# Four edits of order in a hybrid decoder trunk: a weight load's priority, two loads and casts hung behind others, and the bank of two sets of transposes

## The chip, the cores and the metric

The kernel runs on 1 core of one Trainium2 chip. The metric is the device time of one execution in microseconds. The core's engines are named as the profile names them: PE (TensorE, matmuls and transposes; PEld are its weight loads), DVE (VectorE), ACT (ScalarE), POOL (GpSimd) and SP (SyncE), whose queue issues the DMAs here.

## The reference, cut to what matters

One step of a two-layer decoder trunk for 1024 prompt tokens and 8 samples of one token each, D = 1024, in float32:

```python
def trunk(x, p, ...):
    h = x
    for i in range(DEPTH):                       # 2 layers
        hn = rmsnorm(h, norm_mix[i])
        if i % 2 == 0:
            y, S = hgrn2_mixer(hn, ...)          # (o * silu(z)) @ w_out
        else:
            y, vt = chunk_mlp_mixer(hn, ...)     # (u * s * silu(z)) @ w_out, with v = layernorm(gelu(v))
        h = h + y
        gate = sigmoid(rmsnorm(h, norm_ple[i]) @ w_ple_gate[i])
        h = h + gate * (p[i] @ w_ple_proj[i])
    return rmsnorm(h, norm_final), ...
```

Outputs are the trunk's rows, the recurrent states and the normalised v rows of the open chunk.

## The kernel before, in words

Activations lie with features on the partitions. The 1032 tokens are three row blocks c = 0, 1, 2 of 384, 384 and 264 columns (`W`). A weight matrix is walked in tiles of 128 outputs and 1024 inputs. Each product is made in three matmuls (`mm3`, L234): operands are split into a high part, cast by ACT to fp32r, and a low part, the rest, by DVE or POOL; high x high, high x low and low x high are added in one PSUM bank (L236, L237, L238). So a weight tile costs a DMA into `wstg` (two buffers, and a third in some stages), a cast on ACT (`whi`, L150) and a subtraction on DVE (`wlo`, L151) before PE can use it, and two buffers each of `whi` and `wlo` hold the tile in use and the next one.

The wide matrices are done by units (`unit`, L480): a Strassen-like scheme in which two weight tiles together with sums of their quarters (`load_unit`, L185) are multiplied with sums of row blocks 0 and 1; row block 2 is done plainly. Some tiles of each matrix are done plainly throughout.

The order of the work: PE's instructions stand in the order in which the program traces them. Side work is written as generators that are advanced by ticks (`Ticks`, L48) between groups of matmuls. The instructions of the other engines and of SP's queue are ordered by the scheduler when the program is built, greedily: the instruction that is ready with the highest priority goes first. Priority is the place in the program; `tc.high_priority(offset=n)` moves it n places forward (`PRI` is 400), and `tc.issue_after(x)` adds that an instruction on x's engine stands behind x in that engine's queue, without a wait for x to finish.

`order` (L127 to L141) is the list of weight tiles; `take` (L216) hands out one and loads the next one. The places that the change touches:

- **`load` (L167 to L183)**: fetches a tile and splits it. Tiles of the second layer's input matrix ("b"), of the gates ("g") and one half of "p" have their cast and subtraction at high priority; the DMA has none of it.
- **`load_unit` (L185)**: for the first layer's output matrix the key is "Oa" and f is 0 or 1. Its two weight DMAs (L197) have high priority. The first unit, ("Oa", 2, 0), is loaded when the second plain output tile is taken.
- **`last_fill` (L1200)**: the end of the recurrent layer. It makes the second half of p's projection, then loads the gated rows of block 2 for the first half of the output projection: `load_zt` takes four pieces of two rows of 128x264 each from DRAM (`ozd`) through two buffers `zstg` (L385), with a cast (L394) and a subtraction (L398) each. It then takes the first output tile; the plain tiles 0 and 1 of the output projection follow in `out_phase` (L1245).
- **`ple` (L1418)**: the gate stage of each layer. `several(0, 2)` runs tiles 0 and 1 block by block, so that both are used before the next block; then come single tiles. At its head the rows' normalisation (`norm_proc`, L308) is still running: per row j of a block a scaling on DVE (L318), a cast on ACT (L231) and a subtraction (L232), on DVE for odd j and on POOL for even j. A block's normalisation is traced as a whole when its turn comes: block 0's before the first gate group, block 1's within it.
- **`mid` (L1530)**: called before the fourth gate tile of the first layer. It loads the second layer's p rows for all three blocks (`load_p`, L334): DMA, cast L339, subtraction L340. The casts stand behind `last["split"]`, the latest cast of a row. p is used behind the gate stage (`pple`, L352).
- **`vstore` (L1563)**: the second layer's v tiles. Each block of a tile, after its gelu (L1558), is transposed by PE (L1567) into the PSUM tile `pt_g` (tag "pt", one buffer), copied by ACT (L1569), summed for the layer norm (L1572) and stored. Tiles 0 to 3 are done plainly, in pairs block by block (L1578 to L1590), and tiles 4 and up by units. The tag "po" is a bank of its own; the normalisation's sums (`norm_sum`, L284) and the row sums `pr` (L1609) use it too.

Of the kernel before, what the change touches and what calls it, by code (L numbers as in the profile page):

```python
# [8 lines left out]
F32 = mybir.dt.float32  # L9
# [8 lines left out]
P = 128  # L18
# [12 lines left out]
PRI = 400  # L31
# [50 lines left out]
def trunk_kernel(ctx, tc, xT, st, pT, nrm, wina, lbl, gna, wouta, winb, lng, lnb, lngr, lnbr,  # L82
                 wsp, bsp, woutb, wgate, wproj, cst, msk,
                 yT, so_p, so_s, cv_p, cv_s):
    nc = tc.nc
    V, A, G, PE = nc.vector, nc.scalar, nc.gpsimd, nc.tensor
# [3 lines left out]
    def pool(stack, name, bufs=1, **kw):  # L90
        return stack.enter_context(tc.tile_pool(name=name, bufs=bufs, reuse_waits="tile", **kw))
# [5 lines left out]
    pp = pool(ctx, "psum", space=PSUM)  # L97
# [29 lines left out]
    order = [("p", 0, 0), ("a", 8), ("a", 0), ("a", 32), ("a", 33)]  # L127
# [14 lines left out]
    wsrc = {"p": wproj, "a": wina, "z": wina, "oa": wouta, "g": wgate, "b": winb, "ob": woutb}  # L142
# [4 lines left out]
    def split_weights(src, width, names, pl):  # L147
        hi = pl.tile([P, width], F32R, name=names[0], **names[2])
        lo = pl.tile([P, width], F32R, name=names[1], **names[2])
        A.copy(hi, src)  # L150
        last["wnew"] = V.tensor_tensor(lo, src, hi.bitcast(F32), ALU.subtract)  # L151
        return hi, lo

# [6 lines left out]
    def fetch_weights(n):  # L160
        src = wsrc[order[n][0]]
        for i in order[n][1:]:
            src = src[i]
        staged[n] = wp.tile([P, 1024], F32, name="wstg")
        nc.sync.dma_start(staged[n], src)

    def load(n, wait=False):  # L167
        if n >= len(order) or n in loaded or wait and order[n][0] == "B":
            return
        if order[n][0][0].isupper():  # L170
            loaded[n] = load_unit(*order[n])
            return
        if n not in staged:
            fetch_weights(n)
        stg = staged.pop(n)
        with tc.high_priority(offset=PRI if order[n][:2] == ("p", 1) or order[n][0] in ("b", "g") else 0):
            if order[n] in spare:
                hi, lo = loaded[n] = spare[order[n]]()
                split(hi, lo, stg)
            else:  # L180
                loaded[n] = split_weights(stg, 1024, PLAIN, wp)
                if order[n] == ("b", MI + 2):
                    rest["w2"] = last["wnew"]  # L183

    def load_unit(key, m, f=None):  # L185


        a = []
        for _ in range(2):

            third = key != "Z" and nst[0] % 3 == 2
            a.append(ws[0].tile([P, 1024], F32, name="wstg3", bufs=1) if third else
                     wp.tile([P, 1024], F32, name="wstg"))
            nst[0] += key != "Z"
        with tc.high_priority(offset=0 if f is None or (key, m, f) == ("Ob", 4, 0) else PRI):
            for i in range(2):
                nc.sync.dma_start(a[i], wsrc[key.lower()][m + i] if f is None else wsrc[key.lower()][m + i, f])  # L197
        a11, a12, a21, a22 = (a[i][:, j * 512:(j + 1) * 512] for i in range(2) for j in range(2))
        w0 = split_weights(a[0], 1024, PLAIN, wp)
        t = ws[0].tile([P, 512], F32, name="ssum", bufs=2)  # L200
        eng = G if key == "B" else V
        eng.tensor_tensor(t, a21, a22, ALU.add)
        s1 = split_weights(t, 512, SUMS, ws[0])
        eng.tensor_tensor(t, t, a11, ALU.subtract)
        s2 = split_weights(t, 512, SUMS, ws[0])
        t3 = ws[0].tile([P, 512], F32, name="ssum", bufs=2)
        eng.tensor_tensor(t3, a11, a21, ALU.subtract)
        s3 = split_weights(t3, 512, SUMS, ws[0])
        eng.tensor_tensor(t, a12, t, ALU.subtract)
        s4 = split_weights(t, 512, SUMS, ws[0])  # L210
        w1 = split_weights(a[1], 1024, PLAIN, wp)
        return w0, w1, (s1, s2, s3, s4)
# [15 lines left out]
    last, rest = {}, {}  # L228

    def split(hi, lo, src, eng=V):  # L230
        last["split"] = A.copy(hi, src)  # L231
        last["lo"] = eng.tensor_tensor(lo, src, hi.bitcast(F32), ALU.subtract)  # L232
# [139 lines left out]
    def load_zt(zt, parts, stage, n=2, lag=0, tie=True, behind=None):  # L372


        todo = [(ozd[c][:, k0 + k:k0 + k + n, :], *(x[:, k:k + n, :] for x in zt[c, k0][:2]), W[c])
                for c, k0 in parts for k in range(0, zt[c, k0][2], n)]
        return load_list(todo, stage, lag, tie, behind)

    def load_list(todo, stage, lag=0, tie=True, behind=None):

        stg = []
        def fetch(i):
            if i < len(todo):
                stg.append(stage(todo[i][3]))
                last["zt"] = nc.sync.dma_start(stg[i], todo[i][0])  # L385

        for i in range(len(todo) + lag):
            if not lag:
                fetch(i)
            if i >= lag:  # L390
                _, zh, zl, _ = todo[i - lag]
                first = behind and behind()
                with tc.issue_after(first.ins) if first else ExitStack():
                    hi = A.copy(zh, stg[i - lag])  # L394
                if tie:
                    tc.keep_in_program_order(hi)
                with tc.issue_after(rest["sum"].ins) if first and "sum" in rest else ExitStack():
                    V.tensor_tensor(zl, stg[i - lag], zh.bitcast(F32), ALU.subtract)  # L398

            if lag:  # L400
                fetch(i)
            yield

    def stage2(tp, bufs):
        return lambda w: tp.tile([P, 2, 384], F32, name="zstg", bufs=bufs)[:, :, :w]
# [4 lines left out]
    def run(gen):  # L410
        for _ in gen:
            pass
# [770 lines left out]
    zt = {}  # L1183
# [16 lines left out]
    def last_fill():  # L1200
        def halves_of_m():
            while True:
                yield wa.tile([P, 384], F32, name="pple_t", tag="vf", bufs=2)
                t = wa.tile([P, 2, 384], F32, name="pple_t", tag="M", bufs=2)
                yield t[:, 0, :]
                yield t[:, 1, :]

        where = halves_of_m()
        for i, y in enumerate(pple(0, ph, pl, 1, lambda c, mm: next(where)[:, :W[c]])):
            if i == 7:  # L1210
                with tc.issue_after(last["pple"].ins):
                    load(taken[0])
            yield y
        run(load_zt(zt, [(2, 0)], stage2(wa, 2), tie=False))
        assert not any(p[2].__name__ == "reload" for p in tk.procs)
        pre["w"] = take("oa", 0, 0)
        for c in (0, 1):
            pre[c] = pp.tile([P, 512], F32, name="ps_o", tag="mm", bufs=3)
            yield from out_half(pre[c], pre["w"], zt, c, 0)
# [22 lines left out]
    def new_ssq():  # L1242
        return [sp.tile([P, W[c]], F32, name=f"ssq{c}", bufs=1) for c in CH]
# [278 lines left out]
    with ExitStack() as sG:  # L1522
        ep = pool(sG, "pj")
        ssq2 = new_ssq()
        hn = new_act()
        with ExitStack() as s:
            pq = pool(s, "p1", side="right")
            ph, pl = [None] * 3, [None] * 3

            def mid():  # L1530
                behind = last["split"]
                for c in CH:
                    load_p(pq, 1, c, ph, pl, behind, [x[:, :2, :W[c]] for x in xm[c]])

            early = {}
            ple(0, ep, act[0], act[1], ssq2, lambda c: tk.spawn(norm_rows(c, ssq2, 2, (*hn, early), NDEL[1][c])), mid)
            for i, _ in enumerate(pple(1, ph, pl, 0, places([(pq, "pple_t", 8)]))):
                early.setdefault("p", last["pple"])
                if i % 2 or i > 4:
                    tk.tick()  # L1540
# [21 lines left out]

    def vstore(m, c, gv):  # L1563

        pt = pp.tile([P, 3, P], F32, name="pt_g", tag="pt", bufs=1)
        for i in range(NT[c]):
            PE.transpose(pt[:, i, :], gv[:, i * P:(i + 1) * P], ident)  # L1567
        gt = wide().rearrange("p (n e) -> p n e", e=P)
        A.copy(gt[:, :NT[c], :], pt[:, :NT[c], :])  # L1569
        n0 = OFF[c] // P  # L1570
        for i in range(NT[c]):
            V.bn_stats(stats[:, n0 + i, m, :], gt[:, i, :])  # L1572
        nc.sync.dma_start(vraw[m // 2][:, n0:n0 + NT[c], (m % 2) * P:(m % 2 + 1) * P], gt[:, :NT[c], :])
        return
        yield
# [144 lines left out]
    for g in range(8):  # L1720
# [6 lines left out]
        for c in (1, 0, 2):  # L1727
            vn[c] = wb2.tile([P, NT[c], DV], F32, name=f"vn{c}", bufs=1)
            nc.sync.dma_start(vn[c], vraw[g][:, OFF[c] // P:OFF[c] // P + NT[c]])
            for i in range(NT[c]):  # L1730
                n = OFF[c] // P + i
# [12 lines left out]
        else:  # L1744

            zt = {(0, 0): (hh[0], hl[0], 8), (1, 0): (*xm[1], 4), (1, 4): (*xm[0], 4), (2, 0): (hh[2], hl[2], 8)}
# [209 lines left out]
```

## Time and profile before

| what | value |
|---|---|
| median of 3 runs | 1835.99 us (1834.75 to 1836.6) |
| the profiled execution's own time | 1835.75 us |
| its span | 1833.5 us |
| mean granted clock of TensorE | 0.998 |
| HBM read / written | 182.82 MB / 72.80 MB |

The span runs from the first to the last instruction of the program; the execution's own time is 2.25 us longer. A timeline row gives start and duration in us, engine, source line, operation, what it writes and reads, its shape, how many were merged, and in brackets the engine's idle time before it with what ended it. A row of waits gives who waited for whom, and total, times and longest in us. A row of stretches gives the stretch, its length, the busy time and count of PE, PEld, DVE, ACT and POOL, the granted clock, the share of the DMA engines' time, and GB/s. Matmuls are pipelined and their ends are modelled: a matmul's row is longer than the distance to the next one's start, so a short stall of PE doesn't show as idle time.

### The profile page before, as it was taken

How to read it: one execution, taken by the hardware profiler on the slowest of the kernel's cores; microseconds unless marked ns; L12 is line 12 of the kernel's file. 1: busy time of each engine (PE TensorE's matmuls, PEld its weight loads, DVE VectorE, ACT ScalarE, POOL GpSimd, SP SyncE). 2: the span in 40 equal slices, each digit the busy share in tenths (PEclk: the TensorE clock that was granted, in tenths of full speed). 3: DMA queues.
4: the chain of work that ended last, by engine and by line, in shares of the span. 5: the costliest groups of instructions: out<-in, count | busy, mean ns of one | idle time of the engine just before them, and what ended most of it. 6: DMA issues, size and time to landing. Idle time of an engine off the chain costs nothing. (4 is left out here: it accounts for less than half of the span.)

```text
span 1833.5 us, 37336 instructions
## 1 busy us (share of the span) xinstructions
PE 1819.4 (99%) x14542; PEld 1789.5 (98%) x14542; DVE 1364.9 (74%) x2788; ACT 896.2 (49%) x1904; POOL 375.5 (20%) x382
## 2 busy tenths in 40 slices
PE   9999999999999999999999999999999999999998
PEld 8999999999999999999999999999999999999998
DVE  7866888789788886877746755577778877878655
ACT  7533366556656656454435544434434435445442
POOL 0000011111111110000323333354444550000232
PEclk9999999999999999999999999999999999999999
DMA  6233344346444357763254433333334547953222
GB/s 222 80 120 101 114 129 127 112 144 193 142 137 137 106 168 249 264 208 102 61 165 138 124 107 93 97 98 120 115 109 149 174 127 231 308 176 105 90 93 94
DMA packets 167058, 258.06 MB, mean 141 GB/s; under 512 B 16417, under 2 KB 137313, under 8 KB 166881
## 3 DMA queue, kind: packets, MB, share of 16 engines
q1 hardware_dynamic: 166880, 255.68, 44.2%
q8 instruction: 114, 1.87, 0.4%
q14 instruction: 64, 0.52, 0.1%
HBM read 182.82 MB, written 72.80 MB: 139 GB/s over the span
## 5 line engine op out<-in xcount | busy, mean ns | idle before, releaser
L236 PE MATMUL ps_proj<-bh,whi 128*128 128x384 f32 (+1 forms) x2192 | 701.4, 320 | 2.5 <-DVE vl L232 1.2
L237 PE MATMUL ps_proj<-bl,whi 128*128 128x384 f32 (+1 forms) x2192 | 682.7, 311 | 1.9 <-DVE bl L232 1.6
L238 PE MATMUL ps_proj<-bh,wlo 128*128 128x384 f32 (+1 forms) x2192 | 682.6, 311 | 0.0
L236 PEld LDWEIGHTS ps_proj<-bh,whi 128*128 128x128 f32 x2192 | 413.1, 188 | 10.6 <-PE pt_k L1022 3.4
L237 PEld LDWEIGHTS ps_proj<-bl,whi 128*128 128x128 f32 x2192 | 413.6, 189 | 4.5 <-DVE bl L232 4.4
L238 PEld LDWEIGHTS ps_proj<-bh,wlo 128*128 128x128 f32 x2192 | 412.1, 188 | 0.0
L151 DVE TENSOR_TENSOR wlo<-wstg,whi 128x1024 fp32r<-128x1024 f32 x143 | 179.4, 1255 | 99.2 <-ACT whi L150 98.8
L150 ACT CAST whi<-wstg 128x1024 fp32r<-128x1024 f32 x143 | 150.1, 1050 | 144.4 <-PE ps_proj L237 124.1
L150 ACT CAST shi<-ssum 128x512 fp32r<-128x512 f32 x152 | 94.0, 622 | 187.3 <-PE ps_proj L237 89.0
L151 DVE TENSOR_TENSOR slo<-ssum,shi 128x512 fp32r<-128x512 f32 x152 | 110.1, 727 | 4.9 <-ACT shi L150 4.7
L245 POOL TENSOR_TENSOR rsq<-rms_e,mhalf 128x3 f32<-128x3 f32 x15 | 16.4, 1094 | 397.6 <-DVE rms_e L297 397.6
L1008 DVE TENSOR_TENSOR qk<-qk,t 128x384 f32<-128x384 f32 (+1 forms) x144 | 76.6, 536 | 12.1 <-PE pC L958 11.3
L236 PE MATMUL ps_proj<-xmh,shi 128*128 128x384 f32 x244 | 82.7, 339 | 0.0
L238 PE MATMUL ps_proj<-xmh,slo 128*128 128x384 f32 x244 | 81.7, 335 | 0.0
L237 PE MATMUL ps_proj<-xml,shi 128*128 128x384 f32 x244 | 81.6, 335 | 0.0
L236 PE MATMUL ps_o<-bh,whi 128*128 128x384 f32 (+1 forms) x232 | 73.5, 317 | 0.0
L237 PE MATMUL ps_o<-bl,whi 128*128 128x384 f32 (+1 forms) x232 | 72.8, 314 | 0.4 <-DVE bl L398 0.4
L238 PE MATMUL ps_o<-bh,wlo 128*128 128x384 f32 (+1 forms) x232 | 72.7, 313 | 0.0
L1425 DVE TENSOR_TENSOR tmp<-tmp,pj 128x384 f32<-128x384 f32 (+1 forms) x48 | 26.9, 560 | 52.8 <-ACT tmp L1424 49.2
L272 POOL TENSOR_TENSOR ssq<-ssq,tmp 128x384 f32<-128x384 f32 (+1 forms) x36 | 35.0, 972 | 110.8 <-ACT tmp L271 110.8
L245 POOL TENSOR_TENSOR rsq<-ss_e,mhalf 128x3 f32<-128x3 f32 (+2 forms) x32 | 28.7, 897 | 141.1 <-DVE ss_e L1044 137.3
L236 PE MATMUL ps_proj<-bh,shi 128*128 128x384 f32 x164 | 55.9, 341 | 0.0
(396 smaller groups left out, 4210.7 us busy)
## 6 DMA issues: line engine op xcount, KB each, us to landing
wstg<-in_wina SPq DMA_DIRECT2D x48, 512.0 KB, 3.7
wstg<-in_winb SPq DMA_DIRECT2D x48, 512.0 KB, 3.8
pj<-ppd SPq DMA_DIRECT2D x16, 516.0 KB, 4.5
S<-in_st SPq DMA_DIRECT2D x16, 512.0 KB, 3.9
vb<-vd SPq DMA_DIRECT2D x16, 512.0 KB, 4.8
out_so_s<-S SPq DMA_DIRECT2D x16, 512.0 KB, 3.5
wstg<-in_wouta SPq DMA_DIRECT2D x16, 512.0 KB, 3.7
wstg<-in_wgate SPq DMA_DIRECT2D x16, 512.0 KB, 3.7
```

The lines of the kernel that those rows point to most:

```text
L150: A.copy(hi, src)
L151: last["wnew"] = V.tensor_tensor(lo, src, hi.bitcast(F32), ALU.subtract)
L236: PE.matmul(ps, wh, xh, start=first, stop=False, skip_group_check=more)
L237: PE.matmul(ps, wh, xl, start=False, stop=False, skip_group_check=more)
L238: PE.matmul(ps, wl, xh, start=False, stop=last, skip_group_check=more)
L245: G.tensor_tensor(y, e, mhalf[:, :n], ALU.pow)
L272: eng.tensor_tensor(ssq, ssq, sq[:, :w], ALU.add)
L1008: V.tensor_tensor(lev, lev, t2.rearrange("p two (n o) -> p two n o", o=1).broadcast_to([P, 2, n, lv]), ALU.mult)
L1425: V.tensor_tensor(gt[:, :w], gt[:, :w], pj[:, OFF[c]:OFF[c] + w], ALU.mult)
```

## The change

Four edits of order; no arithmetic changes, and no instruction is added or taken away.

- In `load`, gate tiles whose index is 1 (one in each layer) lose the high priority of their cast and subtraction.
- In `load_unit`, the second weight DMA of the first "Oa" unit stands behind the DMA of the last piece that `last_fill` loads for row block 2 (`rest["zt"]`).
- In `mid`, p's casts stand behind the latest cast of a plain weight tile or of a unit's sum (`last["wcast"]`, set in `split_weights`), not behind the latest row cast.
- In `vstore`, block 2 of tiles 1 and 3 is transposed into the bank "po".

```diff
     def split_weights(src, width, names, pl):
...
-        A.copy(hi, src)
+        last["wcast"] = A.copy(hi, src)
         last["wnew"] = V.tensor_tensor(lo, src, hi.bitcast(F32), ALU.subtract)
...
-        with tc.high_priority(offset=PRI if order[n][:2] == ("p", 1) or order[n][0] in ("b", "g") else 0):
+        with tc.high_priority(offset=PRI if order[n][:2] == ("p", 1) or order[n][0] == "b" or
+                              order[n][0] == "g" and order[n][2] != 1 else 0):
...
+        behind = rest.pop("zt", None) if key == "Oa" else None
         with tc.high_priority(offset=0 if f is None or (key, m, f) == ("Ob", 4, 0) else PRI):
             for i in range(2):
-                nc.sync.dma_start(a[i], wsrc[key.lower()][m + i] if f is None else wsrc[key.lower()][m + i, f])
+                with tc.issue_after(behind.ins) if behind and i else ExitStack():
+                    nc.sync.dma_start(a[i], wsrc[key.lower()][m + i] if f is None else wsrc[key.lower()][m + i, f])
...
         run(load_zt(zt, [(2, 0)], stage2(wa, 2), tie=False))
+        rest["zt"] = last["zt"]
...
             def mid():
-                behind = last["split"]
+                behind = last["wcast"]
...
-        pt = pp.tile([P, 3, P], F32, name="pt_g", tag="pt", bufs=1)
+        pt = pp.tile([P, 3, P], F32, name="pt_g", tag="po" if c == 2 and m in (1, 3) else "pt", bufs=1)
```

## The prediction

> **What bounds the kernel now.** I read the page's head first, then the waits of PE alone, then the waits of SP's queue in the stretch of the output projection.
>
> ```profile
> span 1833.5 us, 37336 instructions
> PE 1819.4 (99%) x14542; PEld 1789.5 (98%) x14542; DVE 1364.9 (74%) x2788; ACT 896.2 (49%) x1904; POOL 375.5 (20%) x382
> PE ps_proj L237 <- DVE bl L232: 1.6, 5, 0.5
> PE pt_g L1567 <- ACT u L1569: 0.7, 2, 0.5
> PE ps_o L237 <- DVE bl L398: 0.4, 1, 0.4
> SPq L197 <- DVE wlo L151: 1.6, 1, 1.6
> ```
>
> PE sets the time from end to end: 1819.4 of 1833.5 us. Nothing here can win more than PE's idle moments, and the three waits of PE that the edits aim at (total, times, longest) are a few tenths each. They understate the loss: a matmul's end is modelled, about 0.15 us after its successor can start, so a stall shows as idle only beyond that. I therefore price each stall from start to start, against the same number of matmuls without a stall.
>
> **The row's load ahead of a weight load (load_unit).** PE reaches the third row block of the first output tile at 730.43; five k steps of three matmuls later it is at 732.24, so 0.121 us a matmul and 2.90 us for all 24. The next tile begins at 734.14: 3.71 us, so **0.81 us** are lost.
>
> ```profile
> 730.43 0.28 PE L236 MATMUL ps_o<-bh,whi 128*128 128x264 f32 x1
> 732.24 0.28 PE L236 MATMUL ps_o<-bh,whi 128*128 128x264 f32 x1
> 734.14 0.34 PE L236 MATMUL ps_o<-bh,whi 128*128 128x384 f32 x1
> 725.48 0.33 SPq L197 DMA_DIRECT2D wstg<-in_wouta  x1
> 726.34 0.42 SPq L385 DMA_DIRECT2D zstg<-ozd  x1
> 731.99 0.64 ACT L394 CAST bh<-zstg 128x528 fp32r<-128x528 f32 x1 [5.21 <-DMA zstg<-ozd]
> 732.66 0.71 DVE L398 TENSOR_TENSOR bl<-zstg,bh 128x528 fp32r<-128x528 f32 x1 [4.81 <-ACT bh L394]
> ```
>
> The chain is: the last piece of the row's rows is issued at 726.34, lands 5.6 us later, is cast at 731.99 and split at 732.66 to 733.37, and only then can PE's bl matmul go. It was issued late because the second weight tile of the first wide unit stands before it on SP at 725.48 and had itself waited 1.6 us for a weight buffer. The change puts the piece ahead of that waiting issue, so it can go when the wait begins, near 723.9: 2.4 us earlier, three times what PE lost, if it still takes 5.6 us to land. The moved weight tile loses nothing: its buffer comes free at 725.4 either way, and the piece's own issue (0.42 us) fits into that 1.6 us. Behind the weight tile on SP stand stores and the next tiles' loads; they wait for the same buffer as before. In the DMA engines the weight tile now has a quarter megabyte in front of it; its first reader, the sum of L202, stands on DVE behind the very split that comes 2.4 us sooner, with DVE idle for 4.81 us. Cost of the edit: nothing. Bounds for the gain: 0 (order unchanged) to 0.81; I take 0.81.
>
> **The second gate tile in its turn (load).** At the head of each gate stage PE works on row block 0 while that block's normalised rows are still being split. 24 matmuls and one broadcast of six take 6.04 us from 893.83; the same set takes 4.86 us from 904.76. **1.18 us** are lost, and at the second layer, 6.05 us from 1726.54, **1.19**.
>
> ```profile
> 893.83 0.34 PE L236 MATMUL ps_proj<-bh,whi 128*128 128x384 f32 x1
> 899.87 0.34 PE L236 MATMUL ps_proj<-bh,whi 128*128 128x384 f32 x1
> 904.76 0.33 PE L236 MATMUL ps_proj<-bh,whi 128*128 128x384 f32 x1
> 909.62 0.33 PE L236 MATMUL ps_proj<-bh,whi 128*128 128x384 f32 x1
> 1726.54 0.34 PE L236 MATMUL ps_proj<-bh,whi 128*128 128x384 f32 x1
> 1732.59 0.33 PE L236 MATMUL ps_proj<-bh,whi 128*128 128x384 f32 x1
> 893.90 1.06 ACT L150 CAST whi<-wstg 128x1024 fp32r<-128x1024 f32 x1 [1.21 <-PE ps_o L237]
> 894.86 0.93 ACT L231 CAST bh<-tmp 128x384 fp32r<-128x384 f32 x2
> 894.99 1.22 DVE L151 TENSOR_TENSOR wlo<-wstg,whi 128x1024 fp32r<-128x1024 f32 x1
> 895.86 1.22 POOL L232 TENSOR_TENSOR bl<-tmp,bh 128x384 fp32r<-128x384 f32 x1 [0.77 <-ACT bh L231]
> 896.13 1.36 DVE L232 TENSOR_TENSOR bl<-tmp,bh 128x384 fp32r<-128x384 f32 x1
> 897.42 0.60 DVE L318 SCALAR_TENSOR_TENSOR tmp<-h,g,pbc 128x384 f32<-128x384 f32 x1
> 898.81 0.54 DVE L232 TENSOR_TENSOR bl<-tmp,bh 128x384 fp32r<-128x384 f32 x1
> 894.00:905.00 11.00, 10.56 (x104) 9.46 (x104) 10.95 (x20) 6.77 (x14) 6.58 (x8) 1.00 0.31 95
> 1727.70 1.23 DVE L151 TENSOR_TENSOR wlo<-wstg,whi 128x1024 fp32r<-128x1024 f32 x1
> ```
>
> The gate's second tile, which PE does not read before 899.87, is cast at 893.90 and split at 894.99, in front of the fifth (896.13) and seventh (898.81) row splits that PE is waiting for. DVE has no slack here: 10.95 of 11 us busy. Taking the 1.22 us out of its way and leaving everything else: the scaling of row 7 moves from 897.42 to 895.0 and ends at 895.6, row 5's split follows to about 896.1, row 7's cast on ACT can end near 896.3 and its split near 896.9. Even with the weight's split slipped in between, row 7 is done at about 897.9. PE wants row 7 for its last three matmuls before 899.87, without its stall 1.1 us sooner, so at about 898.3. Both waits go. The tile itself then ends its split at 897.3 to 899 and is wanted at 899.87 + 2 matmuls - 1.18 = 899.0; in the code its load is traced before the first gate group, and row block 1's normalisation inside that group, so at equal priority it still goes ahead of all of row block 1. The edit adds and removes no instruction; it moves the 1.06 us on ACT and 1.22 us on DVE by a few places, and no DMA (the fetch was never inside the priority block). Bounds: 0 to 1.18 for each layer; I take all of it.
>
> A rule against this: POOL does the even rows, and row 5's split took 1.36 us beside POOL's of 895.86, where row 7's took 0.54. [...] That is a rival below.
>
> **What is late next, and p's splits (mid).** If PE arrives 1.2 us earlier, the next closest things in the first layer are the third gate tile and the last row of block 2.
>
> ```profile
> 913.77 0.97 DVE L232 TENSOR_TENSOR bl<-tmp,bh 128x264 fp32r<-128x264 f32 x1
> 916.45 0.28 PE L237 MATMUL ps_proj<-bl,whi 128*128 128x264 f32 x1
> 913.64 1.57 ACT L339 CAST xmh<-pstg 128x768 fp32r<-128x768 f32 x2
> 915.13 1.81 DVE L340 TENSOR_TENSOR xml<-pstg,xmh 128x768 fp32r<-128x768 f32 x2
> 918.43 1.21 DVE L151 TENSOR_TENSOR wlo<-wstg,whi 128x1024 fp32r<-128x1024 f32 x1
> 919.94 0.33 PE L238 MATMUL ps_proj<-bh,wlo 128*128 128x384 f32 x1
> ```
>
> The last row of block 2 is split by 914.74 and read at 916.45: 1.7 us of slack, enough. The third tile's split ends at 919.64 and is read at 919.94: 0.3 us, so by itself the gain of 1.18 would be cut by 0.88. Ahead of that split on ACT and DVE stand p's casts (1.57 us for two of three) and splits (1.81). The change hangs p's casts behind the latest weight cast traced, that of the fourth gate tile, and p's splits follow their casts. Then the third tile depends on PE releasing its buffer, which moves with PE, and keeps the lead. p is not read before the gate stage has run its remaining tiles, so its later place costs nothing; if cover failed, the price would be one of its casts in front of a gate's sigmoid, 0.8 us, with three banks between that and PE. Bounds: -0.88 without the edit, 0 with it. In the second layer nothing of p stands there.
>
> **Transposes in another bank (vstore).**
>
> ```profile
> 1036.91 0.34 PE L238 MATMUL ps_proj<-bh,wlo 128*128 128x384 f32 x1
> 1037.49 0.55 PE L1567 MATMUL pt_g<-ident,u 128*128 128x128 f32 x3 [0.24 <-ACT u L1569]
> 1041.89 0.34 PE L238 MATMUL ps_proj<-bh,wlo 128*128 128x384 f32 x1
> 1042.06 0.49 PE L1567 MATMUL pt_g<-ident,u 128*128 128x128 f32 x3
> 1055.55 0.38 PE L1567 MATMUL pt_g<-ident,u 128*128 128x128 f32 x2
> 1056.39 0.44 PE L1567 MATMUL pt_g<-ident,u 128*128 128x128 f32 x2 [0.46 <-ACT u L1569]
> ```
>
> Two sets of transposes wait until ACT has emptied the single bank of the set before: 0.58 us from matmul to transpose where 0.17 is usual, so **0.41**, and 0.84 for two transposes where a third one costs 0.49 - 0.38 = 0.11, so 0.22 for two and **0.62** lost. Both sets before are the third block of tiles 1 and 3, exactly those that move to the bank "po", which the normalisation has long left and whose next user comes with the row sums after the plain tiles. Bounds 0 to 1.03; I take 1.03.
>
> **Sum.** 0.81 + 1.18 + 1.19 + 1.03 = 4.21 us. The profiled execution took 1835.75 us, 0.24 below the median of the runs, 1835.99. Against the median: 1831.8 us. About 0.2% (3.7 us) is what a measurement of this kernel can tell from no change, so the forecast lies just beyond it and half a microsecond of failure brings it back.
>
> **Rivals.** (1) The weight's split stays where it is. The engines' order is made greedily from what is ready, and the cast at 893.90 started as PE released its buffer, before a row's cast was there: priority may not have put it there. Then 2.37 us stay and only 1.84 go: 1834.2. Against it: after DVE's op before 894.99 the scaling of row 7 was ready and stood behind. (2) Row 7's split, behind the weight's, meets one of POOL's and takes 0.82 us longer, as row 5's did (1.36 against 0.54): 898.7 instead of 897.9, 0.4 us late in each layer, 0.8 less in all, 1832.6. [...] (3) One of the small edits fails, above all the third tile or the early load: 0.8 to 0.9 less, 1832.7. (4) Slower: without priority the second tile falls behind row block 1 altogether. DVE has 0.05 us free up to 905, so its split would end there, while PE wants it at 899.0: 4.8 us more than before at each layer, 9.6 less the 1.84 of the other edits, 1843.8. It decides once the split ends after 900.2, four microseconds later than now; for it speaks that ready work is never held back, against it the order in which the two are traced.
>
> **Chances.** Forecast 0.55, rival (1) 0.12, (2) 0.14, (3) 0.12, (4) 0.05, and 0.02 for nothing at all. The forecast's own range is 1831.1 to 1832.6, from stalls mispriced by half a microsecond and the scatter of the runs shown. Of it some three quarters lie beyond 0.2%, and of (2) and (3) about a third: faster 0.50. Same 0.45, slower 0.05. The range must hold 8 in 10 and so reaches to rival (1): 1830.6 to 1834.4.
>
> **What would show it.** In the profile after, the zstg issue stands before the second L197 and the wait of PE for bl L398 is gone; in both gate stages L151 stands behind at least row 5's split, and the 24 matmuls take about 4.9 us; L339 stands behind two whi casts; PE waits for no u of L1569. I am wrong if PE's first gate group still takes 6 us, if the second gate group begins with a wait for wlo, or if the waits go and the span shrinks by less than 3 us, which would mean that a later wait took them back.

## The result, and the profile after

| kernel | median | runs | profiled execution: span, own time |
|---|---|---|---|
| before | 1835.54 us (1834.28 to 1837.28) | 20 | 1833.5, 1835.75 us |
| after | 1832.68 us (1831.96 to 1833.26) | 20 | 1830.4, 1832.54 us |

The ratio is 0.9984, 95% interval 0.9978 to 0.9990: 2.9 us less, between 1.8 and 4.0. The forecast was 4.21 us less than the runs it started from, 1831.8; the range held the time, but the gain is two thirds of the sum and lies within 0.2%, not beyond it.

All lines of code from the changed places on stand three or four lower in the kernel after (`mm3` is L239 to L241, the row split L235, the transposes L1571). The head of its page and its waits of PE (total, times, longest):

```profile
span 1830.4 us, 37337 instructions
...
PE 1816.0 (99%) x14542; PEld 1787.3 (98%) x14542; DVE 1362.7 (74%) x2788; ACT 895.2 (49%) x1904; POOL 371.3 (20%) x382
```

```profile
PE ps_proj L240 <- DVE bl L235: 1.5, 5, 0.5
...
PE ps_o L239 <- ACT pple_t L367: 0.5, 1, 0.5
```

Of the three waits that the edits aimed at, those for u of the transposes and for the last row's bl (before, L398) are gone. The one for the gate's row splits has lost 0.1 us of 1.6; that row also holds waits between 44 and 50 us that have nothing to do with the gates (0.7 us before, 0.9 after). A wait for a copy of `pple_t` is new.

To see where the time went, I set the two traces beside each other matmul by matmul (PE's order is the same) and measured five stretches, each from the start of one matmul to the start of another, the same two in every kernel. The marks are named by their times before.

| stretch of PE, us | before | after | forecast gain | gain |
|---|---|---|---|---|
| last of the small projection, first plain output tile (700.06 to 734.14) | 34.08 | 33.86 | 0.81 | 0.22 |
| first group of the first gate (890.06 to 900.04) | 9.98 | 9.38 | 1.18 | 0.60 |
| the three groups after it, to the third tile (900.04 to 924.96) | 24.92 | 25.17 | 0 | -0.25 |
| v tiles 0 to 3 (1030.07 to 1060.04) | 29.97 | 28.83 | 1.03 | 1.14 |
| head of the second gate (1724.96 to 1759.93) | 34.97 | 34.49 | 1.19 | 0.48 |
| sum | | | 4.21 | 2.19 |

The span shrank by 3.1 us. The other microsecond is from the first 60 us, where the two programs are the same: the same matmul starts at 60.07 in the profile before and at 59.06 after. The views of stretches show why (stretch, length, busy time and count of PE, PEld, DVE, ACT and POOL, granted clock, share of the DMA engines, GB/s), first of before, then of after:

```profile
44.00:48.00 4.00, 3.17 (x17) 2.16 (x16) 4.00 (x11) 3.42 (x10) 0.00 (x0) 1.00 0.00 0
48.00:52.00 4.00, 3.89 (x19) 3.65 (x19) 3.56 (x8) 2.64 (x7) 0.00 (x0) 0.57 0.02 4
```

```profile
48.00:52.00 4.00, 3.73 (x29) 3.31 (x28) 3.75 (x9) 2.77 (x6) 0.00 (x0) 1.00 0.02 4
```

In the profiled execution of before, TensorE's clock was granted at 0.57 from 48 to 52 us and 19 matmuls were done in place of 29. From 49 us to 60 us, between the same matmuls, it took 11.17 us where the profile after took 9.84, and so lost 1.3 us; the two profiles differ by only 1.0 us because before had been 0.3 us ahead of after until then. None of the eleven other profiles of this study shows the dip (1.00 from 48 to 52 us in each), though the code is the same at this place. It matters below, because the prediction priced a stall 680 us later from this one execution.

The first gate after, in the timeline of PE, then of ACT, DVE and POOL:

```profile
892.75 0.34 PE L239 MATMUL ps_proj<-bh,whi 128*128 128x384 f32 x1
...
897.74 0.44 PE L240 MATMUL ps_proj<-bl,whi 128*128 128x384 f32 x1 [0.30 <-DVE bl L235]
...
898.19 0.34 PE L239 MATMUL ps_proj<-bh,whi 128*128 128x384 f32 x1
...
892.83 1.06 ACT L150 CAST whi<-wstg 128x1024 fp32r<-128x1024 f32 x1 [1.21 <-PE ps_o L240]
893.78 0.92 ACT L234 CAST bh<-tmp 128x384 fp32r<-128x384 f32 x2
...
894.33 0.56 DVE L235 TENSOR_TENSOR bl<-tmp,bh 128x384 fp32r<-128x384 f32 x1 [0.42 <-ACT bh L234]
894.80 0.61 DVE L321 SCALAR_TENSOR_TENSOR tmp<-h,g,pbc 128x384 f32<-128x384 f32 x1
895.33 0.75 DVE L275 TENSOR_TENSOR ssq<-ssq,sql 128x264 f32<-128x264 f32 x1
896.00 1.21 DVE L151 TENSOR_TENSOR wlo<-wstg,whi 128x1024 fp32r<-128x1024 f32 x1
897.13 0.55 DVE L235 TENSOR_TENSOR bl<-tmp,bh 128x384 fp32r<-128x384 f32 x1
...
894.79 1.00 POOL L235 TENSOR_TENSOR bl<-tmp,bh 128x384 fp32r<-128x384 f32 x1 [0.77 <-ACT bh L234]
```

The weight's subtraction (896.00) has moved behind row 5's split (894.33), as forecast, but still stands in front of row 7's (897.13), and PE waits for that one. The first group takes 5.44 us, where 4.86 is undisturbed and 6.04 was before.

### The profile page after: what moved, and what is told of

Its sections match the earlier page's. It is cut to its first block, busy times and chain, and to the rows that moved or that the text cites. A ratio compares the mean times of both kernels' runs of the same rounds, so it can differ in the third digit from the quotient of the medians.

```text
span 1830.4 us, 37337 instructions
## 1 busy us (share of the span) xinstructions
PE 1816.0 (99%) x14542; PEld 1787.3 (98%) x14542; DVE 1362.7 (74%) x2788; ACT 895.2 (49%) x1904; POOL 371.3 (20%) x382
## 4 chain that ended last, share of the span: by engine, by line
PE 91%; DVE 5%; DMA 1%; ACT 1%; issue 1%; POOL 1%; SPq 0%; POOLq 0%; DVEq 0%; ACTq 0%
PE ps_proj L239 22%; PE ps_proj L240 21%; PE ps_proj L241 21%; PE ps_d L241 3%; PE ps_d L239 3%; PE ps_d L240 3%; PE ps_o L239 3%; PE ps_o L240 2%; PE ps_o L241 2%; PE psp L1689 1%; PE pt_g L1571 1%; PE pt_o L1053 1%; PE po L241 1%; PE po L240 1%; PE po L239 1%
## 5 line engine op out<-in xcount | busy, mean ns | idle before, releaser
L239 PE MATMUL ps_proj<-bh,whi 128*128 128x384 f32 (+1 forms) x2192 | 700.6, 320 | 2.7 <-DVE vl L235 1.3
L241 PE MATMUL ps_proj<-bh,wlo 128*128 128x384 f32 (+1 forms) x2192 | 682.1, 311 | 0.0
L239 PEld LDWEIGHTS ps_proj<-bh,whi 128*128 128x128 f32 x2192 | 412.5, 188 | 10.3 <-PE pt_k L1025 3.5
L241 PEld LDWEIGHTS ps_proj<-bh,wlo 128*128 128x128 f32 x2192 | 411.5, 188 | 0.4 <-DVE wlo L151 0.4
L239 PE MATMUL ps_proj<-xmh,shi 128*128 128x384 f32 x244 | 82.7, 339 | 0.0
L241 PE MATMUL ps_proj<-xmh,slo 128*128 128x384 f32 x244 | 81.7, 335 | 0.0
L239 PE MATMUL ps_o<-bh,whi 128*128 128x384 f32 (+1 forms) x232 | 73.4, 317 | 0.5 <-ACT pple_t L367 0.5
L241 PE MATMUL ps_o<-bh,wlo 128*128 128x384 f32 (+1 forms) x232 | 72.7, 313 | 0.0
L239 PE MATMUL ps_proj<-bh,shi 128*128 128x384 f32 x164 | 55.9, 341 | 0.0
```

The lines of the kernel that those rows point to most:

```text
L239: PE.matmul(ps, wh, xh, start=first, stop=False, skip_group_check=more)
L241: PE.matmul(ps, wl, xh, start=False, stop=last, skip_group_check=more)
```

## The experiments

Ten kernels, each profiled and timed beside the kernel before in five rounds. Line numbers differ by up to four from kernel to kernel. The intervals of the ratios reach 1.1 to 2 us to either side, so most differences from row to row lie within them; for these the stretches of PE decide. In the gates and the v tiles these repeat to some hundredths of a microsecond from kernel to kernel wherever the code is the same; the row load's stretch varies more, as shown below. "By place" means read from these stretches, and a tie is one `tc.issue_after`. The last columns are the stretches of the first table in its order.

| kernel | median (before beside it) | ratio, 95% | row load | gate 1, first | gate 1, next | v tiles | gate 2 |
|---|---|---|---|---|---|---|---|
| before | | | 34.08 | 9.98 | 24.92 | 29.97 | 34.97 |
| after | 1832.68 (1835.54) | 0.9984, 0.9978 to 0.9990 | 33.86 | 9.38 | 25.17 | 28.83 | 34.49 |
| early load alone | 1834.57 (1835.30) | 0.9996, 0.9987 to 1.0005 | 34.43 | 9.98 | 24.93 | 29.96 | 34.97 |
| gate edits alone | 1833.85 (1835.30) | 0.9993, 0.9984 to 1.0002 | 34.50 | 9.38 | 25.19 | 29.97 | 34.55 |
| bank alone | 1834.24 (1835.30) | 0.9995, 0.9987 to 1.0004 | 34.51 | 9.99 | 24.93 | 28.83 | 34.98 |
| after, p as before | 1832.43 (1835.30) | 0.9984, 0.9975 to 0.9993 | 33.47 | 9.39 | 25.71 | 28.83 | 34.50 |
| weight behind row 7 | 1832.22 (1834.72) | 0.9985, 0.9976 to 0.9993 | 34.42 | 8.82 | 25.61 | 28.84 | 34.37 |
| and square behind cast | 1831.21 (1834.72) | 0.9981, 0.9972 to 0.9990 | 34.33 | 8.81 | 25.35 | 28.84 | 34.19 |
| copies first | 1831.42 (1834.72) | 0.9982, 0.9973 to 0.9991 | 33.07 | 9.38 | 25.19 | 28.83 | 34.53 |
| the three together | 1830.66 (1834.72) | 0.9976, 0.9967 to 0.9985 | 33.08 | 8.81 | 25.35 | 28.84 | 34.19 |
| and row 0 behind weight | 1829.69 (1835.11) | 0.9971, 0.9960 to 0.9981 | 33.08 | 8.81 | 24.92 | 28.84 | 33.78 |
| three together, no early load | 1832.46 (1835.11) | 0.9985, 0.9976 to 0.9994 | 33.75 | 8.82 | 25.34 | 28.83 | 34.19 |

**The early load alone.** The kernel before, with these hunks:

```diff
+        behind = rest.pop("zt", None) if key == "Oa" else None
...
+                with tc.issue_after(behind.ins) if behind and i else ExitStack():
+                    nc.sync.dma_start(a[i], ...)
...
+        rest["zt"] = last["zt"]
```

> The kernel before with the early load alone. Theory: its gain is real and lies behind the last wait that could take it back: in the stretch of the output projection PE loses 0.81 us before, and after the full change that wait of PE for bl is gone and PE is 0.74 us earlier than the kernel before from there on. So 0.75 us less than before, 0.9996 of its time, and no wait of PE for bl of the row's load. In the profile after, a new wait of PE for ACT's copy of the last pple tile (0.52 us) stands 12 us ahead of it. Theory: that is no doing of the edit; it takes back what PE had won by chance in the first 60 us (0.86 us), because the copy stands on ACT behind a cast that waits for a transfer; here it is there only if PE again arrives early. Rival: the new wait comes with the early load (another order on ACT or SP); then it is here too, whatever PE did before, and the gain is 0.2 us, 0.9999.

```profile
720.03 0.39 PE L238 MATMUL ps_pple<-bh,whi 128*128 128x264 f32 x1 [0.49 <-ACT pple_t L366]
...
721.59 0.44 PE L238 MATMUL ps_o<-bh,whi 128*128 128x384 f32 x1 [0.34 <-ACT pple_t L366]
...
724.39 0.72 SPq L387 DMA_DIRECT2D zstg<-ozd  x1
...
725.87 0.33 SPq L199 DMA_DIRECT2D wstg<-in_wouta  x1
```

The order on SP is the intended one and the wait for the row's bl is gone. PE was at this place 1.3 us earlier than in the profile before, and lost nearly as much in two waits for copies. So the stretch took 34.43 us. That alone doesn't say whose the waits are; the next two kernels do, which have no early load and took 34.50 and 34.51 there. The early load won 0.07 us in these executions, not 0.75: that part of the theory fell.

**The gate edits alone.** The kernel before, with the priority of `load` and `last["wcast"]` in `split_weights` and `mid` as in the change.

> The kernel before with the gate edits alone: the second weight tile at plain priority, p's splits behind the later weight cast. Theory: each gate stage gains about half of what the prediction took, because the weight's subtraction went from in front of row 5's split to in front of row 7's: 24 matmuls in 5.4 us where before had 6.0 and undisturbed ones take 4.9, so 0.60 in each, less 0.21 and 0.11 that PE then waits for the third tile's subtraction: 0.9 us less than before, 0.9995. Rival, the prediction: 2.4 us less, 0.9987. Rival, the meeting with POOL: row 7's subtraction takes 1.36 us instead of 0.54; the theory says that it keeps its 0.55.

```profile
720.34 0.39 PE L237 MATMUL ps_pple<-bh,whi 128*128 128x264 f32 x1 [0.43 <-ACT pple_t L365]
...
721.91 0.44 PE L237 MATMUL ps_o<-bh,whi 128*128 128x384 f32 x1 [0.35 <-ACT pple_t L365]
...
719.50 0.51 ACT L395 CAST bh<-f 128x384 fp32r<-128x384 f32 x1 [0.69 <-DMA f<-ozd]
719.92 0.37 ACT L365 COPY pple_t<-ps_pple 128x264 f32<-128x264 f32 x1
721.07 0.51 ACT L395 CAST bh<-f 128x384 fp32r<-128x384 f32 x1 [0.78 <-DMA f<-ozd]
721.48 0.65 ACT L365 COPY pple_t<-ps_pple 128x264 f32<-128x264 f32 x2
...
897.71 0.55 DVE L233 TENSOR_TENSOR bl<-tmp,bh 128x384 fp32r<-128x384 f32 x1
```

The first gate group gains 0.60 and the three groups after it lose 0.27; the second gate's head gains 0.42: 0.75 by place, near the theory's 0.9 and far from 2.4. Row 7's split keeps its 0.55 us; it is late, not long. The waits for copies at 720 to 722 are here too, without the early load; each copy stands on ACT behind a cast that waited for a transfer (0.69 and 0.78 us).

**The bank alone.** The kernel before, with the tag of `vstore`.

> The kernel before with the transposes' other bank alone. Theory and prediction agree: both waits of PE for u go in full, 0.41 and 0.62, so 1.03 us less than before, 0.9994, and no wait for pt_g in the profile. Rival: the row sums that use the bank next wait for ACT to empty it, and give back what was won; then 0 to 0.5 us, and a new wait of PE within 5 us behind the last of these transposes.

The waits for u are gone, the stretch of the v tiles is 1.14 us shorter, and behind it nothing is given back.

**After, p as before.**

```diff
...
-                behind = last["wcast"]
+                behind = last["split"]
```

> The kernel after with p's casts tied as before, everything else changed. Theory, as the prediction priced it: p's casts and splits stand in front of the third gate tile's again; three of DVE's (0.96, 0.96, 0.69) come ahead of that tile's subtraction, which ends about 0.8 us later than PE wants it, so 0.7 us more than after, in the first layer alone, and PE is late at the head of the third tile by 0.9 instead of 0.2. Rival: p's place costs nothing, since ACT and DVE have gaps of 1.1 to 1.6 us at that point in the profile after; then the same as after.

```profile
916.30 0.69 DVE L343 TENSOR_TENSOR xml<-pstg,xmh 128x528 fp32r<-128x528 f32 x1
916.92 1.21 DVE L151 TENSOR_TENSOR wlo<-wstg,whi 128x1024 fp32r<-128x1024 f32 x1
...
918.19 0.44 PE L241 MATMUL ps_proj<-bh,wlo 128*128 128x384 f32 x1 [0.51 <-DVE wlo L151]
```

p's last subtraction stands straight in front of the weight's, and PE waits for it at the third tile. The three groups take 0.54 us more than after (25.71 against 25.17), somewhat below the theory's 0.7. The medians differ by 0.25 us the other way, which is less than they can tell; by time alone the edit would have passed for worthless.

**The weight's subtraction behind row 7's split.** After, and in `split_weights` and `load` for the second gate tile:

```diff
-    def split_weights(src, width, names, pl):
+    def split_weights(src, width, names, pl, behind=None):
...
-        last["wnew"] = V.tensor_tensor(lo, ...)
+        with tc.issue_after(behind.ins) if behind else ExitStack(): last["wnew"] = V.tensor_tensor(lo, ...)
...
-                loaded[n] = split_weights(stg, 1024, PLAIN, wp)
+                loaded[n] = split_weights(stg, 1024, PLAIN, wp, last["lo"] if order[n][0] == "g" and order[n][2] == 1 else None)
```

> The kernel after, and in both gate stages the second tile's subtraction is tied behind row 7's split. Theory: this is what the prediction left in. On DVE row 7's split follows row 0's scaling of block 1 and ends near 897.05 instead of 897.68, so the first 24 matmuls take 4.9 us, not 5.4: 0.5 us. But the weight's subtraction then ends at 898.2, where PE would want it at 897.95, and the third tile's, at the end of a chain of ACT casts and squares, stays where it is: there PE already waits 0.2 and 0.1 us, and would be 0.3 to 0.5 earlier. So the gain is taken back 21 us later, the wait moves from bl to wlo, and the time is that of after, 0.9984 of before. Rival: the third tile's chain moves up with PE, then 1.0 us less than after, 0.9979.

```profile
895.21 0.60 DVE L321 SCALAR_TENSOR_TENSOR tmp<-h,g,pbc 128x384 f32<-128x384 f32 x1
895.74 0.55 DVE L235 TENSOR_TENSOR bl<-tmp,bh 128x384 fp32r<-128x384 f32 x1
896.20 1.21 DVE L151 TENSOR_TENSOR wlo<-wstg,whi 128x1024 fp32r<-128x1024 f32 x1
...
897.01 0.33 PE L240 MATMUL ps_proj<-bl,whi 128*128 128x384 f32 x1
897.47 0.44 PE L241 MATMUL ps_proj<-bh,wlo 128*128 128x384 f32 x1
```

The first group is whole again (8.82, 1.16 less than before). Then PE stands between 897.01 and 897.47, where a matmul is due every 0.17 us: it now waits for the second tile's subtraction, 0.38 us at this and the next matmul together. The row of PE shows no wait; the view of the waits of PE's weight loads does:

```profile
PEld ps_proj L241 <- DVE wlo L151: 1.4, 4, 0.5
```

Over both groups of rows 0.56 is won and 0.44 given back in the first layer, 0.12 is left in the second. That the wait moves to wlo was right, the place was not: the second tile takes most of it back, and the third tile's chain, which I had held to be fixed, moved up with PE.

**And the square behind the third tile's cast.** In addition, in `group`:

```diff
+            with tc.issue_after(last["wcast"].ins) if (m, c) == (1, 1) else ExitStack(): accum_sq(sp, ssq[c], ...)
```

> As the run with the subtraction behind row 7, and in both gate stages the square of the second tile's middle block, which waits on ACT for DVE, goes behind the third tile's cast. Theory: the cast goes 1.0 us earlier (915.0 instead of 916.05 in the profile after), the third tile's subtraction ends ahead of PE, and what the first tie won stays: 0.3 to 0.5 in each stage and the 0.2 and 0.1 that after lost there, so 0.9 to 1.3 us less than after, 0.9978 of before. Rival: the square's delay makes DVE's sum of squares or the bank late, and PE waits for a bank in the second or third tile instead; then as after.

```profile
914.21 1.05 ACT L150 CAST whi<-wstg 128x1024 fp32r<-128x1024 f32 x1
915.17 0.52 ACT L274 ACTIVATE tmp<-h 128x384 f32<-128x384 f32 x1
...
917.20 0.34 PE L240 MATMUL ps_proj<-bl,whi 128*128 128x384 f32 x1
917.38 0.33 PE L241 MATMUL ps_proj<-bh,wlo 128*128 128x384 f32 x1
```

In the profile after the two stood the other way round:

```profile
915.62 0.52 ACT L274 ACTIVATE tmp<-h 128x384 f32<-128x384 f32 x1 [0.60 <-DVE h L1430]
916.05 1.03 ACT L150 CAST whi<-wstg 128x1024 fp32r<-128x1024 f32 x1
```

The cast no longer waits behind a square that waits for DVE, and the third tile starts without a gap: 0.26 and 0.18 us by place. Against after, the gates have gained 0.39 and 0.30, below the 0.9 to 1.3 expected of both, since the wait for the second tile's subtraction is still there.

**Copies first.** After, and in `pple`:

```diff
-                with tc.high_priority(offset=0 if half and not l else PRI), tc.issue_after(gone.ins) ...:
+                with tc.high_priority(offset=PRI), tc.issue_after(gone.ins) ...:
```

> The kernel after, and the copies that empty the banks of the second half of the small projection ahead of the output projection have priority on ACT over the casts that wait for a transfer. In six profiles so far PE passes that place (720 to 722 us) with 0 to 1.2 us of waiting for such a copy, the more the earlier it comes; and PE's wait for the last row's split, 11 us later, is shorter by as much. Theory: the copy behind a cast on ACT is the cause; with the copies first the bank waits go and, since the early load has the row there in time, PE keeps what it won before: 0.6 us less than after by its profile (0.2 to 1.2), 0.9980 of before. Rival: the rows' transfers set the time of this stretch; the first of the last two pieces is issued some 3 us later in this order, and PE waits for its split near 731 instead: as after, 0.9984.

```profile
719.26 0.38 ACT L367 COPY pple_t<-ps_pple 128x264 f32<-128x264 f32 x1 [1.05 <-DMA ppd<-pple_t]
719.54 1.15 ACT L397 CAST bh<-f 128x384 fp32r<-128x384 f32 x2
...
719.75 0.42 PE L239 MATMUL ps_o<-bh,whi 128*128 128x384 f32 x1
```

The copy stands ahead of the two casts, PE's waits for copies are gone, and the stretch takes 33.07 us: 0.79 less than after, and 1.3 to 1.4 less than the five executions in which both waits stood. So the order on ACT was the cause: it is all that the edit changes, and no wait for the rows' transfers took the gain back.

**The three together.** Both ties and the copies first.

> The two ties and the copies first together. Theory: the gains are of different places and add, 0.9 to 1.3 and 0.6: 1.5 to 1.9 us less than after, 0.9975 of before. Rival: one of them is taken back at a later wait, then 0.9979 to 0.9984.

The gains are of different places and add: by the table 0.78, 0.57, -0.18 and 0.30, 1.47 us less than after. The medians differ by 2.0 us and the ratios by 0.0008, which is 1.5 us.

**And row 0 behind the weight.** In addition, in `norm_proc`:

```diff
+            with tc.issue_after(last["wnew"].ins) if (c, j) == (1, 0) else ExitStack(): V.scalar_tensor_tensor(t[:, :w], src(j), ...)
```

> As the run with everything together (two ties and copies first), and in both gate stages the scaling of row 0 of block 1, which had slipped in front of row 7's split on DVE, is tied behind the second tile's subtraction. In that run the first 24 matmuls took 4.9 us, but PE then waited 0.4 us for the second tile's subtraction. Theory: the head of the gate is a queue on DVE in which each operation that stands ahead shows on PE; with 0.53 us less ahead of it the subtraction ends before PE wants it, and the first 48 matmuls take twice 4.9 us: 0.4 less in each layer, 0.8 in all, 0.9972 of before. Rival: the delay of row 0 moves on through row block 1, which DVE also does without a gap, and PE waits at the third group, 10 us later, for a row of that block: then as the run with everything together, 0.9976.

```profile
894.88 0.55 DVE L235 TENSOR_TENSOR bl<-tmp,bh 128x384 fp32r<-128x384 f32 x1
895.35 1.22 DVE L151 TENSOR_TENSOR wlo<-wstg,whi 128x1024 fp32r<-128x1024 f32 x1
...
891.63 0.34 PE L239 MATMUL ps_proj<-bh,whi 128*128 128x384 f32 x1
...
896.50 0.33 PE L239 MATMUL ps_proj<-bh,whi 128*128 128x384 f32 x1
...
901.39 0.33 PE L239 MATMUL ps_proj<-bh,whi 128*128 128x384 f32 x1
```

With row 0's scaling out of the way the subtraction ends at 896.57, before PE wants it, and the first two groups take 4.87 and 4.89 us. Both gates now have all that the prediction had promised them: 9.98 to 8.81 and 34.97 to 33.78, 1.17 and 1.19, with 24.92 for the groups between, as before. Row block 1 doesn't suffer. This is the fastest version, 1829.69 us, 0.9971 of before (0.9960 to 0.9981).

**The three together, without the early load.** `behind = None` in `load_unit`.

> As the run with everything together, without the early load: the row's last piece goes behind the second weight load again. Theory: the early load is worth something only where PE arrives early enough; with the copies first PE is at the third row block 0.8 us sooner than after, the piece lands some 1.8 us later than in the run with everything together (there split by 729.3, wanted near 730.5), so PE waits about 0.5 us for bl near 731, and the time is 0.5 to 1.0 us more than that run, 0.9980 of before. Rival: the early load is worth nothing once the copies are first, the time is the same, 0.9976.

```profile
723.88 0.43 SPq L200 DMA_DIRECT2D wstg<-in_wouta  x1
724.36 0.43 SPq L388 DMA_DIRECT2D zstg<-ozd  x1
...
730.76 0.71 DVE L401 TENSOR_TENSOR bl<-zstg,bh 128x528 fp32r<-128x528 f32 x1 [1.64 <-ACT bh L397]
...
731.52 0.39 PE L240 MATMUL ps_o<-bl,whi 128*128 128x264 f32 x1 [0.36 <-DVE bl L401]
```

The last piece goes out behind the weight tile and PE waits for its split: 33.75 us against 33.08, 0.67 by place, as the theory had it. The early load is worth this once the copies don't take PE's lead first. By time the run was 1.7 us slower than the three together (0.9985 against 0.9976), more than the 0.5 to 1.0 expected; the two intervals overlap, and by place nothing else differs by more than 0.01.

## Why the prediction was right or wrong, point by point

**The early load: mechanism right, size wrong.** The step that failed is "3.71 us, so 0.81 us are lost": true of the one execution, which had lost 1.3 us in the dip of the clock at 48 to 52 us. An execution that comes on time loses its lead 12 us earlier, waiting for copies that stand on ACT behind casts which wait for transfers (0.43 and 0.35 us with the gate edits alone), and finds the row's split nearly ready. The two waits stand in series, and only the one that PE meets first shows. Over the executions without copies first the stretch took 34.08, 34.50 and 34.51 without the early load, and 33.86, 34.43, 33.47, 34.42 and 34.33 with it: 34.36 against 34.10 in the mean, some 0.3 us with that much scatter, and 0.67 with the copies out of the way. The stall itself can be read apart from the copies, from the first matmul of the third row block to the next tile: 3.71 us before, but 3.03 and 2.90 with the gate edits and the bank alone, which have no early load, 2.90 in every kernel with it, and 3.57 with the copies first and no early load. So where both copy waits stood only 0.13 and 0 us of the 0.81 were left to win. The prediction's list of waits that would be late next had none ahead of the edit's own place.

**The second gate tile: 0.60 instead of 1.18, and again in the second layer.** The sentence "Both waits go" failed. The prediction let row 7's scaling run ahead of row 5's split, "from 897.42 to 895.0", which is 893.9 in the clock of the profile after; it ran at 894.80. The greedy order took row 5's split first, and that one waited 0.42 us for its cast, because ACT still cast the weight ahead of it: the priority was gone, but row 5's scaling ended only at 892.84, as PE released the weight's buffer, so the cast of the weight (892.83) was the first that could start. Row 7 was done 0.86 us later than the 897.9 of the prediction, at 897.68 in the profile after, 0.5 after PE wanted it. So rival (1), the split staying where it is, was half of what happened: it stayed in front of one row of the two. The last two ties show the full 1.17 and 1.19 us: the price of the stall was right, and what was missing was where the weight's subtraction has to stand, behind row 7's split and ahead of row 0's scaling.

**Rival (2), the meeting with POOL, did not come.** Row 5's split took 0.56 us at 894.33, where 1.36 was before, and POOL's next split (894.79) began only near its end; row 7's took 0.55. That POOL's split beside it made the 1.36 us was the author's estimate from that pair, 1.36 and 0.54; no run shows it by itself, and it decided nothing here.

**p's splits: right in kind.** The prediction took 0 with the edit and -0.88 without it, for a PE 1.18 us earlier. With PE 0.60 earlier the runs gave -0.25 with and -0.79 without (25.17 and 25.71 against 24.92). The remainder with the edit is one that the text had not listed: the third tile's cast stood behind a square on ACT which waited for DVE, and the tie of the square took it away.

**The transposes: right**, 1.14 for 1.03, with nothing given back at the bank's next user.

**The sum.** 2.19 by place, where 4.21 was forecast: 0.59 short in the early load, 0.83 in the first gate, 0.71 in the second, 0.11 over in the transposes. The measured 2.9 (1.8 to 4.0) agrees with it. It is also the time of rivals (2) and (3), 1832.6 and 1832.7, though neither alone is what happened: the time doesn't tell these accounts apart, the stretches do. The prediction's own sign of being wrong, a span that shrinks by less than 3 us, was escaped by luck: 1.0 of the 3.1 us came from the dip of the clock. Nothing pointed to the slower rival: row block 1 was never in the weight's way. Why the first of the two copy waits is there in five executions and not in those of before, after, and after with p as before I have not settled; in the five the cast ahead of the copy waited 0.67 to 0.82 us for its transfer, in the other three for none.

## What to carry to other kernels

A stall in one profiled execution is priced for that execution's phase: before you count it, look whether PE came to it late, and ask which wait it would meet first if it came on time. Taking priority from an operation doesn't say where it goes; if its new place matters, tie it to the two operations it has to stand between. An engine that empties a bank should not have an instruction that waits for a transfer in front of the copy: with the copies in front the row load's stretch took 33.07 us, without 33.86.

## What the runs showed of the hardware

In one profiled execution out of twelve, that of before, the granted clock of TensorE fell while it had work: to 0.57 in the mean from 48 to 52 us, 0.50 from 48.5 to 51.5, which cost 1.3 us. Just before, from 44 to 48 us, PE had been busy for 3.17 of 4 us at a clock of 1.00, with waits of half a microsecond at most (0.24 and 0.48); the other eleven passed the same place at 1.00, with 3.06 to 3.18 us busy from 44 to 48. What made the clock fall is not shown. At the end of the program, where PE has nothing left to do, it falls in both profiles, before and after. In before PE's last matmuls ran from 1826.14 to 1826.97 us, and the clock was 1.00 up to 1830.0 and 0.50 from 1830.5 on; in after they ran from 1823.03 to 1823.86, and it was 1.00 up to 1827.5 and 0.50 from 1828.0 to 1831.0.
